# A rotation kernel: its first 1 MB load issued in three parts over strided partitions, its last store in two

## The chip, the cores and the metric

One core of one Trainium2 chip. The time is the device time of one execution in microseconds; lower is better. The six runs of the kernel before lie within 0.3% of each other. Verdicts of faster or slower are taken at 2%; intervals are 95% intervals.

## The reference

```python
x = np.random.randn(32, 3, 256, 256).astype(np.float32)     # seeded
out = np.rot90(x, k=-1, axes=(-2, -1))
```

96 images of 256 x 256 float32, each turned by 90 degrees: 25.17 MB in, 25.17 MB out, no arithmetic.

## The kernel before

The images are cut into 12 slabs of 2 MB. Each slab has its own buffer, so no load waits for a buffer to come free (most of the later loads wait, up to 2.0 us each, until an earlier transfer has landed). VectorE transposes slab n into the buffer of slab n-1, which is then stored; slab 0 goes through PSUM and is copied by ScalarE into a buffer that has come free, so it is stored last. SyncE issues every load, then every store.

```python
    for n in range(n_slabs):
        if n == last:
            nc.sync.dma_start(out=units[n], in_=ld8_v[n])
            continue
        for i in range(I):                                    # I = 2: two loads of 1 MB
            if n == 0:
                nc.sync.dma_start(out=units[n][:, i], in_=ld8_v[n][:, i])      # 128 partitions x 8 KB
            else:
                nc.sync.dma_start(out=units[n][i::I].rearrange("p i f -> p (i f)"), in_=ld16_v[n, i])
    # ... transposes on VectorE, stores of slabs 1 to 11 (cut) ...
    for i in range(I):
        nc.scalar.copy(out=units[last][:, i], in_=turned0[:, i])
    nc.sync.dma_start(out=st_v[0], in_=units[last])
```

## Time and profile before

| | kernel before |
|---|---|
| median of 6 runs | 123.99 us (123.74 to 124.13) |
| span in the profile | 122.2 us |
| moved, and mean rate over the span | 50.33 MB, 412 GB/s |
| rate in the steady part | 428 to 430 GB/s |
| VectorE busy | 93.3 us, done at 99 us |
| first packet starts | 1.74 us |

How to read it: this kernel only moves data, so the row to look at is the one of the 16 DMA engines. The profile's lines, and what they leave to win, are in the prediction.

### The profile page before, as it was taken

The page shows a single profiled execution, that of the slowest core. Times are in us where ns is not written, and L with a number is a line of the kernel's source. Part 1 is how long each engine was busy: PE and PEld are TensorE (multiplying, and loading weights), DVE is VectorE, ACT ScalarE, POOL GpSimd, SP SyncE. Part 2 cuts the span into 40 slices and gives each one's busy share as a digit, 9 for nine tenths or more (in the row PEclk, how much of TensorE's full clock was granted, in tenths as well). Part 3 has the DMA queues.
Part 4 walks back from the last instruction along what each step waited for, and adds up shares of the span by engine and source line. Part 5 has one row for each costly group of instructions (what it writes and reads, how often), then busy time and mean ns, then how long its engine had stood idle before and what let it go on. Part 6 is the DMA issues. An engine that isn't in the chain of part 4 may idle for free.

```text
span 122.2 us, 134 instructions
## 1 busy us (share of the span) xinstructions
DVE 93.3 (76%) x24; ACT 5.0 (4%) x3; POOL 0.2 (0%) x4
## 2 busy tenths in 40 slices
DVE  0299999999999999999999999999999940000000
ACT  0000000000000000000040000000000651000000
POOL 0000000000000000000000000000000000000000
DMA  3999999999999999999999999999999999999993
GB/s 88 429 432 434 440 440 429 429 429 429 429 429 429 429 429 424 434 424 408 370 414 428 426 429 429 429 429 429 429 429 429 424 429 429 429 429 426 429 429 166
DMA packets 5584, 50.33 MB, mean 412 GB/s; under 512 B 592, under 2 KB 720, under 8 KB 848
## 3 DMA queue, kind: packets, MB, share of 16 engines
q1 hardware_dynamic: 5584, 50.33, 97.8%
HBM read 25.17 MB, written 25.17 MB: 412 GB/s over the span
## 4 chain that ended last, share of the span: by engine, by line
DMA 57%; DVE 13%; issue 7%; DVEq 3%; ACT 2%; SPq 1%
DMA u<-in_x_dram 39%; DMA out_dram<-u 18%; DVE u L82 10%; DVE u L76 3%; DVEq L119 3%; ACT u L92 2%; SPq L66 1%; SPq L89 0%
## 5 line engine op out<-in xcount | busy, mean ns | idle before, releaser
L82 DVE STREAM_TRANSPOSE u<-u 128x2048 f32<-128x2048 f32 x20 | 78.0, 3948 | 0.3
L76 DVE STREAM_TRANSPOSE turned<-u 128x2048 f32<-128x2048 f32 x2 | 7.6, 3828 | 5.5 <-DMA u<-in_x_dram 5.5
L76 DVE STREAM_TRANSPOSE u<-u 128x2048 f32<-128x2048 f32 x2 | 7.8, 3953 | 0.0
L92 ACT COPY u<-turned 128x2048 f32<-128x2048 f32 x2 | 3.7, 1866 | 33.8 <-DVE u L76 33.8
L92 ACT ACT_TABLE_LOAD x1 | 1.3, 1283 | 62.4 <-DMA u<-in_x_dram 62.4
L108 POOL MEMSET const-bfloat16-1.0<- 128x1 bf16 x1 | 0.1, 102 | 0.0
L108 POOL MEMSET const-uint8-127<- 128x1 uint8 x1 | 0.1, 102 | 0.0
L108 POOL MEMSET const-float32-0.0<- 128x1 f32 x1 | 0.1, 99 | 0.2 <-issue 0.2
L108 POOL MEMSET const-float32-1.0<- 128x1 f32 x1 | 0.1, 99 | 0.0
## 6 DMA issues: line engine op xcount, KB each, us to landing
u<-in_x_dram SPq DMA_DIRECT2D x22, 1024.0 KB, 19.6
out_dram<-u SPq DMA_DIRECT2D x11, 2048.0 KB, 25.0
u<-in_x_dram SPq DMA_DIRECT2D x1, 2048.0 KB, 22.5
out_dram<-u SPq DMA_DIRECT2D x1, 1024.0 KB, 20.2
out_dram<-u SPq DMA_DIRECT2D x1, 896.0 KB, 20.2
out_dram<-u SPq DMA_DIRECT2D x1, 128.0 KB, 20.6
```

The lines of the kernel that those rows point to most:

```text
L66: nc.sync.dma_start(out=units[n][:, i], in_=ld8_v[n][:, i])
L76: nc.vector.transpose(out=dst[:, :, ::-1, ::-1], in_=src)
L82: nc.vector.transpose(out=dst[:, cs], in_=src[:, cs])
L92: nc.scalar.copy(out=units[last][:, i], in_=turned0[:, i])
L108: nc = _bacc.Bacc("TRN2", target_bir_lowering=False, num_devices=1)
L119: with _tile.TileContext(nc) as tc:
```

## The change

Intent: the first load is cut so that fewer rows (of 8 KB, one packet each) stand ahead of those of the engines that start late, which the author supposed would shorten the ramp of the first 3 us. Every fourth partition is taken, and not 32 neighbours. The last store is cut so that its first half can be issued ahead of the second copy.

```diff
             if n == 0:
-                nc.sync.dma_start(out=units[n][:, i], in_=ld8_v[n][:, i])
+                for ps in (slice(0, P, 4), slice(2, P, 4), slice(1, P, 2)) if i == 0 else (slice(0, P),):
+                    nc.sync.dma_start(out=units[n][ps, i], in_=ld8_v[n][ps, i])
...
     for i in range(I):
         nc.scalar.copy(out=units[last][:, i], in_=turned0[:, i])
-    nc.sync.dma_start(out=st_v[0], in_=units[last])
+        nc.sync.dma_start(out=st_v[0][:, i], in_=units[last][:, i])
```

## The prediction

> **What bounds the kernel now.** I read the page first: the busy shares and the 40 slices, to see whether an engine or the transfers run without a break.
>
> ```profile
> span 122.2 us, 134 instructions
> DVE 93.3 (76%) x24; ACT 5.0 (4%) x3; POOL 0.2 (0%) x4
> ...
> DVE  0299999999999999999999999999999940000000
> ...
> DMA  3999999999999999999999999999999999999993
> GB/s 88 429 432 434 440 440 429 429 429 429 429 429 429 429 429 424 434 424 408 370 414 428 426 429 429 429 429 429 429 429 429 424 429 429 429 429 426 429 429 166
> DMA packets 5584, 50.33 MB, mean 412 GB/s; under 512 B 592, under 2 KB 720, under 8 KB 848
> ```
>
> The transfers are the bound: the DMA row is 9 in every slice but the first and last, at 429 GB/s nearly throughout. VectorE stops at 99 us while the transfers go on for 20 us more. 50.33 MB at 429 GB/s take 117.3 us (my arithmetic), so 4.9 us of the span of 122.2 are something else: the start, the end, and the dip of slices 19 to 21, where loads give way to stores.
>
> Next the DMA queue's own waits from 95 us on, for the end:
>
> ```profile
> SPq L119 <- DMA out_dram<-u: 19.7, 1, 19.7
> SPq L89 <- DVE u L76: 7.3, 1, 7.3
> SPq L93 <- ACT u L92: 1.4, 1, 1.4
> ```
>
> The last store is issued at 101.15 us (timeline of SyncE) and lands some 20 us later. It is not late; it stands behind a backlog. The chain of waits lists DVE and ACT pieces (L82, L76, L92) because it follows who released whom; with 20 us of stores queued behind them those pieces set nothing.
>
> Last, the windows, drawn finely around the start. Columns: stretch, length, DVE, ACT, POOL busy, clock, DMA share, and GB/s, which counts a packet in the stretch in which it starts.
>
> ```profile
> 0.00:1.70 1.70, 0.00 (x0) 0.00 (x0) 0.20 (x4) 1.00 0.00 0
> 1.70:1.90 0.20, 0.00 (x0) 0.00 (x0) 0.00 (x0) 1.00 2.13 328
> 1.90:2.00 0.10, 0.00 (x0) 0.00 (x0) 0.00 (x0) 1.00 0.00 0
> 2.00:2.10 0.10, 0.00 (x0) 0.00 (x0) 0.00 (x0) 1.00 1.32 164
> 2.10:2.35 0.25, 0.00 (x0) 0.00 (x0) 0.00 (x0) 1.00 0.00 0
> 2.35:2.55 0.20, 0.00 (x0) 0.00 (x0) 0.00 (x0) 1.00 0.95 328
> 2.55:2.70 0.15, 0.00 (x0) 0.00 (x0) 0.00 (x0) 1.00 0.00 0
> 2.70:2.80 0.10, 0.00 (x0) 0.00 (x0) 0.00 (x0) 1.00 1.35 573
> 2.80:3.00 0.20, 0.00 (x0) 0.00 (x0) 0.00 (x0) 1.00 0.68 287
> 3.00:3.20 0.20, 0.00 (x0) 0.00 (x0) 0.00 (x0) 1.00 1.16 492
> 3.20:5.40 2.20, 0.00 (x0) 0.00 (x0) 0.00 (x0) 1.00 1.01 428
> ```
>
> GB/s times length over 8192 bytes (one row, one packet here) gives packets: 8 start in 1.70 to 1.90 us, 2 at 2.0, 8 in 2.35 to 2.55, then 7, 7 and 12, so 44 by 3.20 us. Of the 16 engines, 8 start on time, the other 8 about 0.65 us later, and the early ones move next to nothing meanwhile: 2 second packets. At the full rate 16 packets go in 0.306 us (16 x 8192 B at 428 GB/s). If 16 first packets started at once at t0, the 44th would have started about 28 packets on, at t0 + 0.54 us; so the stream is where it would be had it begun in full at 2.66 us less a mean half packet of 0.15: about 2.5 us. It began at 1.74. **About 0.75 us is lost in the ramp**, and this is the only thing the first part of the change can win.
>
> [...] the existing loads of every second partition run at 430 GB/s (window 5.40 to 55), so a stride of 2 costs nothing. [...] 592 packets under 512 B are 16 for each of 37 transfers. [...]
>
> **The change, part by part.**
>
> *First load in three.* It removes one transfer of 128 rows and adds three of 32, 32 and 64. Bytes and data packets stay. [...] The full stream then begins near 1.9 to 2.0 us instead of 2.5: **0.5 us gained**, 0.6 to 0.7 at best.
>
> Can the next transfers keep up? L66 issues take 0.39 and 0.42 us plus 0.05 (chain of waits), so parts are issued at 0.73, 1.17, 1.61, the second half at 2.05, later ones every 0.5. First packets come 1.0 us after an issue begins. Part 1 has 2 packets an engine (0.61 us), part 2 the same, part 3 four (1.22 us). Starting at 1.95, part 1 runs to 2.55; part 2 can begin at 2.17 to 2.35; it runs to 3.2; part 3 can begin from 2.6 to 2.95; the second half from 3.05 to 3.7 and is needed at 4.4. It keeps up, tightest at part 2 (0.2 us). No loss, unless the early stall repeats for each part; then 0.1 to 0.3 us comes back off.
>
> *Two more issues* on SyncE, 0.45 us each: all else is issued about 0.9 us later in the first microseconds, hidden under a queue of several MB.
>
> *The last store in two.* The first 1 MB half no longer waits for the second copy (1.87 us, ending at 101.13), so it may be issued after the previous store, at about 99.7. Both halves still stand behind about 19 us of queued stores: **0 us**.
>
> *Three more transfers* add 48 semaphore packets, 3 an engine. Loads carry one such packet per 64 KB and engine, most stores one per 128 KB, yet both run at 428 to 430 GB/s; 0.5% of 2.44 us is 0.01 us each, so at most 0.03 us.
>
> VectorE begins when the first half has landed, about 0.4 us sooner; with 20 us of slack at the end this counts for nothing. Sum: 0.5 gained, 0.03 lost, and 124.06 becomes about **123.55 us**.
>
> **The rivals.** *The stall is the cold first access, not descriptors.* Half of the engines stall about 1 us on a first or second packet[...]. For it: the stall ends everywhere around 2.7 to 2.9. Against it: two engines finish a first packet in 0.3 us and stall in the second, and the late eight don't stall. Then nothing is gained: 124.0. *The split feeds too slowly*: each 256 KB part has a ramp of its own, the engines run dry between, the gain is used up and 0.1 to 0.3 us lost: 124.2 to 124.4. Against it: the sum above has each part ready in time. *Everything up to the first microsecond is recovered*, the smaller first issue also being shorter and the end less ragged (GB/s falls over about 0.7 us as the engines finish one by one): 123.1. [...] half speed on 1 MB would cost 2.4 us (126.5); the full rate of stride-2 loads speaks against it.
>
> **Range and chances.** The three runs of before spread over 0.14 us, so the noise is small beside the gain. I give the descriptor story about two in three, the cold-access one one in four. From 123.1 (all recovered) to 124.05 (nothing recovered) should hold 8 in 10. Two per cent would be 2.48 us, more than three times the ramp's whole loss; the tail and the dip, about 2 us more, are not addressed. Faster by over 2%: 0.01. [...]
>
> **What would show it.** Right: in the windows of the start, 16 packets start within about 0.3 us of the first instead of 8, and the full rate holds from about 2.0 us with no hole up to 5; the first transpose starts near 5.0 instead of 5.5; the DMA row is 9 everywhere as before; the last stores still land 20 us after their issue. 640 packets under 512 B. Wrong: the same hole between 1.9 and 2.35 us (cold access), or new holes at 2.5, 3.2 or 4.4 us (feeding), or a first load at half the rate [...]. The whole prediction is wrong if the gain at the start is lost at the dip near 60 us, where loads and stores meet.

The sum came to 123.55 us (124.06 - 0.5 + 0.03; the slip is dealt with below). The 0.5 us was the author's estimate from the windows of before: 8 engines start 0.65 us late; if they wait for the 64 rows of the other half of the transfer, that is 10 ns a row; with 32 rows in all they would wait for 16, which is 0.16 us; and the stall of the early engines was expected to shrink alike. That engines wait for rows is not shown; this supposition is what the text calls "the descriptor story". Cut too is the sentence that gave slower by over 2% a chance of 0.01, if the strided parts ran at a lower rate.

## The result, and the profile after

The changed kernel takes **125.75 us** (median of 6 runs, 125.13 to 126.20) against 123.99 us. The ratio is 1.014, interval 1.0106 to 1.0174: slower by 1.4%, clear of the noise, and outside the predicted range. Ratios are computed as the mean time of one kernel's runs over that of the other's of the same rounds, so they are not quite the ratios of the medians that are quoted.

The page of the changed kernel, the lines that answer to those of before:

```profile
span 123.9 us, 139 instructions
DVE 93.3 (75%) x24; ACT 5.0 (4%) x3; POOL 0.2 (0%) x4
...
DVE  0069999999999999999999999999999950000000
...
DMA  3899999999999999999999999999999999999992
GB/s 90 294 426 423 428 434 434 423 439 428 434 428 423 434 423 428 434 423 413 379 392 425 426 434 426 428 431 423 431 426 426 428 431 428 428 428 423 431 421 124
DMA packets 5632, 50.33 MB, mean 406 GB/s; under 512 B 640, under 2 KB 768, under 8 KB 896
```

Busy times are the same, and so is the steady rate. The second slice has fallen from 429 to 294 GB/s. The ramp that was to become shorter has become longer.

The windows of the start, in the stretches that the prediction used (the last column counts a packet where it starts):

```profile
1.70:1.90 0.20, 0.00 (x0) 0.00 (x0) 0.00 (x0) 1.00 0.00 0
...
2.00:2.10 0.10, 0.00 (x0) 0.00 (x0) 0.00 (x0) 1.00 2.31 410
2.10:2.35 0.25, 0.00 (x0) 0.00 (x0) 0.00 (x0) 1.00 2.18 360
2.35:2.55 0.20, 0.00 (x0) 0.00 (x0) 0.00 (x0) 1.00 0.00 0
2.55:2.70 0.15, 0.00 (x0) 0.00 (x0) 0.00 (x0) 1.00 0.00 0
2.70:2.80 0.10, 0.00 (x0) 0.00 (x0) 0.00 (x0) 1.00 0.39 164
2.80:3.00 0.20, 0.00 (x0) 0.00 (x0) 0.00 (x0) 1.00 0.97 410
3.00:3.20 0.20, 0.00 (x0) 0.00 (x0) 0.00 (x0) 1.00 1.38 533
3.20:5.40 2.20, 0.00 (x0) 0.00 (x0) 0.00 (x0) 1.00 0.72 250
```

GB/s times length over 8192 bytes: 5 packets in the first of these stretches with any and 11 in the second. All 16 engines now start within 0.3 us, where before 8 started and 8 followed 0.65 us later. That is what the prediction hoped for. But they start at 2.04 us and not at 1.74, and no second packet starts before 2.7 us: each first packet takes 0.65 to 0.92 us, where one of 8 KB takes 0.31 us later on. In the kernel before, too, 14 of the 16 engines end their first packet only between 2.7 and 3.0 us. By 3.20 us 41 packets have started, against 44. So far nothing is won and little lost. Then comes the last line: 250 GB/s where before had 428.

Coarser windows of the kernel before, and then of the changed one, show how far the hole reaches:

```profile
2.70:3.80 1.10, 0.00 (x0) 0.00 (x0) 0.00 (x0) 1.00 1.02 432
3.80:5.30 1.50, 0.00 (x0) 0.00 (x0) 0.00 (x0) 1.00 1.01 426
5.30:8.00 2.70, 2.50 (x1) 0.00 (x0) 0.00 (x0) 1.00 1.06 449
8.00:20.00 12.00, 11.97 (x4) 0.00 (x0) 0.00 (x0) 1.00 1.00 427
20.00:55.00 35.00, 34.83 (x10) 0.00 (x0) 0.00 (x0) 1.00 1.01 430
```

```profile
2.70:3.80 1.10, 0.00 (x0) 0.00 (x0) 0.00 (x0) 1.00 1.02 387
3.80:5.30 1.50, 0.00 (x0) 0.00 (x0) 0.00 (x0) 1.00 0.55 180
5.30:8.00 2.70, 0.67 (x1) 0.00 (x0) 0.00 (x0) 1.00 1.01 404
8.00:20.00 12.00, 11.96 (x4) 0.00 (x0) 0.00 (x0) 1.00 1.02 433
20.00:55.00 35.00, 34.83 (x10) 0.00 (x0) 0.00 (x0) 1.00 1.01 429
```

The DMA share falls to 0.55 between 3.8 and 5.3 us: nearly half of the engines have no packet. The three stretches together lack (432-387) x 1.1 + (426-180) x 1.5 + (449-404) x 2.7 = 540 KB, which at 429 GB/s is 1.26 us; the next one, to 20 us, gives 72 KB back, so 1.1 to 1.26 us are missing. From 20 us on the rate is the same in both.

The single packets of the trace show what happens in the hole. Six engines pass from part 2 to part 3 without a break, at 3.76 to 3.89 us. The other ten are empty for 0.3 to 1.5 us and get their first packet of part 3 at 4.27 to 5.31 us (the trace does not number the engines; they are told apart by which packet starts where another ends). From 3.2 to 8 us an engine is empty for 0.61 us in the mean. In the same time its packets take 0.42 us more than they would at the usual 0.309 us for 8 KB and 0.611 us for 16 KB. In the kernel before both are zero. So engines that have nothing to do are the larger part of the loss, and slow packets around the gap are the smaller.

The issues of these loads, before (first line) and after, with the duration of one in ns (shortest, median, longest):

```profile
L66 SPq DMA_DIRECT2D u<-in_x_dram x2: 389/406/422, 0.7 to 1.2; - x2
```

```profile
L68 SPq DMA_DIRECT2D u<-in_x_dram x4: 542/579/587, 0.7 to 2.6; - x4
```

The very first issue, now to 32 strided partitions, takes 0.54 us, not 0.39: fewer rows, but a longer issue. The fourth of them, the second half of the slab, is the same transfer to 128 consecutive partitions as before, and it too takes 0.58 us where it took 0.42. So here the same transfer took 0.16 us longer to issue behind three strided parts than behind one load of 128 partitions.

The loss shows again at the end of the span. The windows there, before and after:

```profile
119.50:120.20 0.70, 0.00 (x0) 0.00 (x0) 0.00 (x0) 1.00 0.94 398
120.20:120.90 0.70, 0.00 (x0) 0.00 (x0) 0.00 (x0) 1.00 0.29 117
```

```profile
120.20:120.90 0.70, 0.00 (x0) 0.00 (x0) 0.00 (x0) 1.00 1.00 421
120.90:121.50 0.60, 0.00 (x0) 0.00 (x0) 0.00 (x0) 1.00 0.65 273
121.50:122.00 0.50, 0.00 (x0) 0.00 (x0) 0.00 (x0) 1.00 0.47 197
122.00:122.50 0.50, 0.00 (x0) 0.00 (x0) 0.00 (x0) 1.00 0.35 147
```

The end is ragged: engines run out of work one by one over more than 1.5 us. It comes from the start. For each transfer the trace has the moment at which each of the 16 engines reports its share landed. Before, those 16 moments lie within 0.26 us for the first load, 0.25 us at 57 us, and 0.62 us at the end. After, they lie 1.72 us apart for the third part (5.48 to 7.20 us), 1.78 us at 57 us, and 1.98 us at the end. From 12 us to the dip near 60 us the 16 moments of each transfer keep their distances within about 0.1 us, and after the dip again, so the same engines are still late 115 us later (an inference, as the engines have no names): every transfer has a landing from each of the 16, and with a DMA share of 1.01 from 20 to 55 us and from 62 to 119.5 us none of them idles to let a late one catch up. The loss is complete by 10 us. For the second half of slab 0 the mean of the 16 moments is 8.95 us against 7.79, and the last of them 9.91 against 7.93: 1.16 and 1.98 us later. At the end of the span it is 122.16 against 120.84 in the mean and 123.09 against 121.18 for the last: 1.32 and 1.91 us later.

### The profile page after: what moved, and what is told of

Read it like the earlier page. It is cut to its first block, busy times and chain, and to the rows that moved or that the text cites. A ratio compares the mean times of both kernels' runs of the same rounds, so it can differ in the third digit from the quotient of the medians.

```text
span 123.9 us, 139 instructions
## 1 busy us (share of the span) xinstructions
DVE 93.3 (75%) x24; ACT 5.0 (4%) x3; POOL 0.2 (0%) x4
## 4 chain that ended last, share of the span: by engine, by line
DVE 46%; issue 27%; DMA 4%; DVEq 3%; ACT 2%; SPq 1%
DVE u L84 37%; DVE turned L78 6%; DMA u<-in_x_dram 4%; DVE u L78 3%; DVEq L121 3%; ACT u L94 2%; SPq L68 1%; DVEq L78 0%
```

## The experiments

Twelve experiments with eleven kernels (one was run twice), each with runs of the kernel before on the same chip. All but the store-only kernel have the last store whole, as before. The theory (F): a part holds too little work, and the engines run dry before the packets of the next part are there. Rivals: S, the loss is made by the store at the end; K, strided partitions are slow wherever they stand.

### Which half of the change

The load in three parts alone:

```diff
-        nc.sync.dma_start(out=st_v[0][:, i], in_=units[last][:, i])
+    nc.sync.dma_start(out=st_v[0], in_=units[last])
```

> The load in three parts alone, the last store whole as before. Theory F (the small parts run the transfer engines dry before the next part's packets are there): all of the loss is here, 125.4 to 126.1 us, the same hole of about 1 us between 3.8 and 5.3 us, and the landings of one transfer over the engines spread by about 1.7 us. Rival S (the loss is at the end, from the last store in two): back to 123.7 to 124.1 us.

Measured: 125.47 us against 123.80, ratio 1.0139 (1.0107 to 1.0171). The rate between 3.8 and 5.3 us is 235 GB/s and that from 5.3 to 8 us 322; landings are 1.9 us apart at 57 us (its profile is of the slowest of four runs, 126.19 us). The whole loss is in the load.

The last store in two alone (the load as before):

> The last store in two alone, the load as before. Theory F: 123.8 to 124.2 us, nothing gained or lost, since both halves stand behind some 19 us of queued stores. Rival S: 125 us or more, with the ragged end of 1.5 us that the changed kernel shows.

Measured: 123.81 us against 123.80, ratio 0.9992 (0.9977 to 1.0007). The store does nothing. Rival S has fallen.

### How large a part, and in which order

Two parts of 64 partitions in place of three:

```diff
-                for ps in (slice(0, P, 4), slice(2, P, 4), slice(1, P, 2)) if i == 0 else (slice(0, P),):
+                for ps in (slice(0, P, 2), slice(1, P, 2)) if i == 0 else (slice(0, P),):
```

> The first load in two parts of 64 strided partitions, the store whole. Theory F: a part now holds 4 packets an engine (1.2 us) against about 0.6 us from issue to issue, so the hole closes: 123.4 to 124.2 us. Rival K (a transfer to strided partitions has its packets delivered slowly, however large it is; all 128 rows are strided here too): the hole stays, 125 us or more.

Measured: 124.88 us, ratio 1.0069 (1.0034 to 1.0104): between the two expectations. Half of the loss is gone, not all. From 3.8 to 5.3 us the rate is 404 GB/s, so the large hole has closed, but the second half of the slab arrives late on some engines (two of the 16 spend 1.23 and 1.27 us on one 8 KB packet of it), and landings are 1.06 us apart at 57 us. Here hardly any engine is empty after 3.2 us (0.05 us in the mean), so slow packets and a late start make this loss, not engines that have nothing to do.

The same three parts, the large one first:

```diff
+                for ps in (slice(1, P, 2), slice(0, P, 4), slice(2, P, 4)) if i == 0 else (slice(0, P),):
```

> The same three parts, the one of 64 partitions first, the store whole. Theory F: 1.2 us of packets an engine stand ready when the two small parts are issued, so most of the hole closes: 123.5 to 124.6 us. Rival K, or a fixed cost of about 0.6 us for each extra transfer: as slow as with the small ones first, 125.2 to 126 us.

Measured: 124.40 us, ratio 1.0037 (1.0018 to 1.0056). Same transfers, same count, same stride; the order alone takes back nearly three quarters of the loss. That speaks for F and against a fixed cost for each part. What is left of the loss is again slow packets (0.44 us an engine from 3.2 to 8 us), with no engine empty.

The first small part, then the whole second half (1 MB), then the other two:

```diff
+            for ps, i in ((slice(0, P, 4), 0), (slice(0, P), 1), (slice(2, P, 4), 0), (slice(1, P, 2), 0)):
+                nc.sync.dma_start(out=units[n][ps, i], in_=ld8_v[n][ps, i])
```

> The same four transfers of slab 0, reordered: the first small part, then the whole second half (1 MB), then the other two parts; the store whole. Theory F: the small part is followed by 2.4 us of work, so the later parts come in time: 123.8 to 124.6 us. If each of the three strided parts costs by itself: 125.2 to 126 us, as with all three ahead.

Measured: 124.23 us, ratio 1.0024 (1.0006 to 1.0042), as F expects. This trace also measures the delivery. The 1 MB transfer is issued at 1.32 us; the engines finish the small part from 2.75 us on, and some then wait: 11 of 16 are busy at 3.1 and all at 3.5 us. Its first packets start at 2.76 and 2.78 us on two engines and at 3.08 to 3.42 on the others. Its packets thus came 1.4 to 2.1 us after its issue began, not 1.0 us as for the first transfer of the kernel before.

Slab 1 first (2 MB), then slab 0 in the three parts:

```diff
-    for n in range(n_slabs):
+    for n in (1, 0, *range(2, n_slabs)):
```

> The two 1 MB loads of slab 1 first, then slab 0 with its first half in the same three strided parts; the store whole. Theory F (parts hurt only while the engines have no queue behind them): 2 MB, about 5 us of work, stand ahead of the parts, so no hole: 123.4 to 124.3 us, the landings of one transfer within 0.4 us over the engines. Rival K (strided parts are slow wherever they stand): 125 us or more.

Measured: 123.85 us against 123.93, ratio 0.9991 (0.9959 to 1.0022). The windows of this run:

```profile
3.80:5.30 1.50, 0.00 (x0) 0.00 (x0) 0.00 (x0) 1.00 0.83 350
5.30:8.00 2.70, 0.00 (x0) 0.00 (x0) 0.00 (x0) 1.00 0.99 419
8.00:20.00 12.00, 8.94 (x3) 0.00 (x0) 0.00 (x0) 1.00 1.02 433
```

The parts' own packets run from 7.5 to about 10.2 us here, in stretches of 419 and 433 GB/s (the 350 counts packets of 16 KB by their start, and no engine was idle there). The very same strided transfers, with 2 MB in front of them, cost nothing. One expectation was missed: the landings lie 0.65 us apart, not within 0.4. Rival K has fallen as the whole cause: stride is not slow wherever it stands. Whether the parts' packets were delivered just as late here, hidden behind the 2 MB, this run can't tell.

### Stride and smallness apart

Strided, but nothing small: slab 0 in two transfers of 1 MB, each over every second partition.

```diff
+            for j in range(2):
+                nc.sync.dma_start(out=units[n][j::2], in_=ld8_v[n][j::2])
```

> Slab 0 in two transfers of 1 MB as before, but each over every second partition (64 partitions, both halves of the row): strided partitions without any small transfer. If the stride costs only a later first packet (2.05 us instead of 1.75) and a longer issue (0.55 us instead of 0.39), and 1 MB of work covers the next issue: 123.7 to 124.3 us, no hole after 3.2 us. If the stride itself starves the engines: 125 us or more.

Measured: 124.32 us against 123.90, ratio 1.0035 (1.0020 to 1.0051), just above the range. Its issues take 0.71 and 0.61 us and its first packet starts at 2.21 us. Its windows:

```profile
2.70:3.80 1.10, 0.00 (x0) 0.00 (x0) 0.00 (x0) 1.00 0.74 246
3.80:5.30 1.50, 0.00 (x0) 0.00 (x0) 0.00 (x0) 1.00 1.00 426
```

The first packets come late (246 GB/s where before had 432), and then there is no hole. This version costs 0.4 us. That this is the price of the stride is not shown: the run with slab 1 first also begins with transfers over every second partition (64 rows of 16 KB, issues of 0.55 and 0.58 us), its first packet starts at 2.06 us, and it lost nothing.

Small, but not strided: three parts of the same sizes, cut by columns, over all 128 partitions.

```diff
+                for cs in (slice(0, F // 4), slice(F // 4, F // 2), slice(F // 2, F)) if i == 0 else (slice(0, F),):
+                    nc.sync.dma_start(out=units[n][:, i, cs], in_=ld8_v[n][:, i, cs])
```

> The first half in three parts of the same sizes (256, 256, 512 KB), but each over all 128 partitions, cut by columns (rows of 2, 2 and 4 KB). If what costs is that a small transfer holds too little work (theory F): the same hole, 125 to 126.5 us, more if packets are made row by row. If it is the stride over partitions (rival K): the issue takes 0.4 us as before, no hole, 123.7 to 124.3 us.

Measured: 124.63 us against 123.93, ratio 1.0053 (1.0017 to 1.0088): neither expectation. Its windows:

```profile
2.70:3.80 1.10, 0.00 (x0) 0.00 (x0) 0.00 (x0) 1.00 0.90 253
3.80:5.30 1.50, 0.00 (x0) 0.00 (x0) 0.00 (x0) 1.00 1.08 348
```

The issues take 0.39 to 0.43 us, as K said, and the first packet comes at 1.74 us, but the rate from 2.7 to 5.3 us is low, so small parts cost without stride too. The share beside it says that this is mostly not for want of packets: 14 of the 16 engines have one from 2.7 to 3.5 us and 13 to 16 after that; the packets, of 2 and 4 KB, take longer than usual (103 to 121 ns in the mean for 2 KB, where the median is 84). So this run does not isolate size. The two versions cost 0.7 and 0.4 us and the three strided parts 1.7, more than the sum; but as neither run isolates its cause the sum proves nothing.

### Issuing from two queues

As the load-only kernel, but the second part and the second half are issued by ScalarE:

```diff
+                    eng = nc.scalar if (i, j) in ((0, 1), (1, 0)) else nc.sync
+                    eng.dma_start(out=units[n][ps, i], in_=ld8_v[n][ps, i])
```

> The three parts as in the changed kernel, but the second part and the second half are issued from ScalarE's queue, so that SyncE issues half as many in the ramp; the store whole. If the pace of issues on SyncE (0.61 us each) is what starves the engines: most of the hole closes, 123.7 to 124.6 us. If it lies behind the issue, in what both queues share: 125 us or more, hole as before.

Measured: 124.08, 123.97, 125.55 and 124.13 us against 123.93; ratio 1.0031, interval 0.9970 to 1.0092. Three of four runs are within 0.2 us of before, and in the profiled one the stretch from 3.8 to 5.3 us moves 437 GB/s; one run is as slow as the changed kernel. So with the third part and the second half both issued at 1.3 us instead of 1.95 and 2.58 the hole is usually closed, but not reliably; the interval holds a loss of 0.9% as well as none.

The control: no parts, the second half from ScalarE (ScalarE in place of SyncE for `i == 1`).

> The kernel before with the second half of slab 0 issued from ScalarE's queue at the same moment as the first from SyncE, no parts. A control for the two-queue run with parts: if two queues shorten the ramp by themselves, 123.3 to 123.7 us; if they only save issue time that was hidden, 123.8 to 124.1 us, the same as before.

Measured: 123.74 us against 123.90, ratio 0.9987 (0.9973 to 1.0001). That lies between the two expectations. Two queues save nearly nothing by themselves; in three of the four runs with parts they gave back most of what the parts had cost.

### Fewer transfers instead of more

Slab 0 in one transfer of 2 MB:

```diff
+            nc.sync.dma_start(out=units[n], in_=ld8_v[n])
```

> Slab 0 in one transfer of 2 MB, fewer transfers instead of more. Theory F: the engines are never dry in either, and the ramp is that of a 128-partition issue: 123.6 to 124.1 us, no change. A rival in which every transfer issued in the ramp costs time of its own: 0.3 us or more faster than before.

Measured: 123.77 us against 123.93, ratio 0.9980 (0.9952 to 1.0008). Again, with more rounds:

> The kernel with slab 0 in one 2 MB transfer again, with more rounds, to decide whether its 0.2% are real: ratio 0.997 to 1.000 to the kernel before; it would be the one version that beats both.

Measured: 123.76 us against 123.90, ratio 0.9985 (0.9972 to 0.9998). It is the fastest version with the clearest sign, by 0.15%, hardly a gain. All 16 engines have a packet by 2.0 us in it, earlier than in the changed kernel and with 256 rows in the transfer, and again the full rate comes only after 3 us.

| slab 0's first transfers | first one | ratio to before |
|---|---|---|
| 32, 32, 64 strided partitions, 128 | 256 KB | 1.0139 |
| 64, 64 strided, 128 | 512 KB | 1.0069 |
| 64, 32, 32 strided, 128 | 512 KB | 1.0037 |
| two of 64 strided, both halves | 1 MB | 1.0035 |
| 32 strided, 128, 32 and 64 strided | 256 KB, then 1 MB | 1.0024 |
| the three parts behind 2 MB of slab 1 | 1 MB | 0.9991 |
| one of 128 | 2 MB | 0.9985 |

The fifth row shows that with a small first transfer and a large one at once behind it little was lost (1.0024).

**What stays open.** In the changed kernel the third part is issued at 1.95 us and its packets start between 3.8 and 5.3 us, 1.8 to 3.4 us later. The runs show that this delivery is late and that with 2 MB in front of the parts nothing is lost (0.9991). They do not show why the lag grows from 1.3 us for the first transfer to 3.4 us, or why packets around a gap take longer; the traces have no view of what happens between an issue and its first packet. One more sign is in the issues: the one that SyncE begins at 4.37 us, in the hole, lasts 1.30 us, and 1.68 us in the load-only run, where in the kernel before none of the first ten lasts over 0.61 us. So issues were held up in the same stretch as packets; which of the two is the cause, or whether both have one, is not shown.

## Why the prediction was wrong

**The bound** was right. The DMA row is full as before except in the second slice, VectorE now starts at 7.3 us and not at 5.5, and this costs nothing: with slab 1 first it started at 11.0 us and the time was that of before.

**The gain of 0.5 us at the ramp** failed. The staggered start did vanish (all 16 engines within 0.3 us). That few rows were the reason is not shown: the one 2 MB transfer has 256 rows and no such stagger either. And the stall behind it did not shrink alike. The engines' second packets start at 2.7 to 3.1 us (two of before excepted) whether the first ones came from 1.74 on (before) or from 2.04 on (after), and with 16 packets started by 2.0 us (one 2 MB transfer) the full rate comes no earlier. The rival "the stall is the cold first access", given one chance in four, fits this in so far as the stall ends at about the same time in both kernels; what makes the stall is not shown.

**"It keeps up, tightest at part 2 (0.2 us). No loss"** is the step that made the number wrong. It rests on two figures taken from the unsplit load. "L66 issues take 0.39 and 0.42 us": for the parts and the half behind them they measured 0.54 to 0.59. "First packets come 1.0 us after an issue begins": 1.32 us for the first part, and 1.8 to 3.4 us for the third, which was expected "from 2.6 to 2.95" and came from 3.8 to 5.3; ten engines ran dry while they waited for it. The rival "the split feeds too slowly" was the right one, but its 0.1 to 0.3 us were too small: the engines lost 1.16 us in the mean by the second half, and the latest of them 1.98 us. It had left out that the engines could fall behind by different times and stay so to the end (landings 1.72 us apart for the third part, 1.98 us at the end).

**Strided parts at half speed**: not seen. The stride-only run loses its 0.4 us ahead of 3.8 us and then runs at 426 GB/s, and behind 2 MB the parts cost nothing. **The sum** has a slip: 124.06 - 0.5 + 0.03 is 123.59, not 123.55; nothing hangs on it.

**The last store in two, 0 us**: right (0.9992). **Three more transfers, at most 0.03 us**: 640 semaphore packets were counted as foreseen; the store-only run, with one more transfer, shows no cost. **The dip near 60 us** took nothing back. **Chances**: within 2% was right; the range (to 124.05) did not allow for a loss at all.

## What to carry to other kernels

Here the three parts cost 1.4% with nothing in front of them and nothing (0.9991) behind 2 MB. At the start the time from issue to packets was 1.4 to 3.4 us for the transfers behind the first, more than the first one's own lag of 1.0 us suggests. So set the work queued in front of a transfer against that time: let the first or the second transfer be large (here 1 to 2 MB) and cut later ones if at all. Where the engines never idle, as here after the start, look at the spread over engines and not only at the mean rate: it was 1.7 us at 7 us and still 2.0 us at the end. When a figure is borrowed for a transfer of another shape (here the issue time), treat it as open until a trace shows it.
